# Prefetch hints with the routing bit ahead of every branch of the expert part, and PLE products staged in five buffers in place of two

## The chip, the cores and the metric

The kernel runs on one core of a Trainium2 chip. The metric is the device time of one execution in microseconds (us); the time of a kernel is the median of its timed runs. All durations below are from one profiled execution of the kernel before, by the hardware profiler.

## The reference

One layer of a decoder trunk over 2048 tokens of width 1024, in float32. A mixer (a gated MLP over positions and a gated recurrence) comes first, then a mixture of experts, then a per-layer embedding (PLE) gate and a final norm. The part that the change touches is the mixture and the PLE product:

```python
def hier_moe(h, w_grp, w_exp, w1, w3, w2):
    # top-1 group of 4, then top-2 experts of the 8 inside it: 32 experts, 2048 tokens x 2
    ...
    def expert_block(args):
        xb, e = args
        return (jax.nn.silu(xb @ w1[e]) * (xb @ w3[e])) @ w2[e]

    ybuf = lax.map(expert_block, (buf.reshape(n_blk, MOE_BLOCK, D), blk_e)).reshape(P, D)
    contrib = ybuf[dest] * w_s[:, None].astype(xt.dtype)
    out = jax.ops.segment_sum(contrib, tok_s, num_segments=T)
    return out.reshape(B, S, D)
...
        x = x + merged @ w_out[i]
        h = rmsnorm(x, g_ffn[i])
        x = x + hier_moe(h, w_grp[i], w_exp[i], w1[i], w3[i], w2[i])
        h = rmsnorm(x, g_ple[i])
        x = x + jax.nn.sigmoid(h @ w_pg[i]) * (p[i] @ w_ple[i])
    return rmsnorm(x, g_final)
```

w1 and w3 of an expert are 1024 x 512 each, w2 is 512 x 1024, so an expert brings 6.29 MB of weights. `p[i] @ w_ple` is 2048 x 256 by 256 x 1024; it depends on no routing.

## The kernel before

The program is straight-line code, unrolled, except for the branches named here. Its stages, one behind the other: the mixer with the routing; a stretch in which the routing table is scattered to HBM (`tab_d`), read back (`tokidx`), and the rows of the first experts are gathered; the 32 experts; the final tiles.

**The experts.** Each expert takes its first 128 tokens with split products: ACT makes `ehi` (a rounded copy of a weight piece), DVE makes `elo` (the rest), and PE multiplies three products of two halves each, `P0` to `P7` for the eight pieces of w1 and w3 (L903, six matmuls a piece), then `B0` to `B3` for w2 (L935). `ehi` and `elo` have five buffers each (`SPL`). `x` (L877) and `y` (L881) split the tokens' columns `xr`, which `X` (L852) turns out of the gathered `rows`. The order is written out by hand in the string `PART`: one pass of it for an expert has the second half of the expert before (`S T G B Y`), the first half of this one (`P`, with `h`, `l`, `v`, `u` for ehi and elo), and the first splits of the next one (`X x y H L`). Inside one engine the instructions run in this order and no other.

**The branches.** At the end of each pass stands, on every engine, `tc.If` on a bit of the routing code (L1095): has the expert more than 128 tokens? If so, `some(0)` does the next 32 with plain products (L948, a transpose L954, L959); a second bit (L1097) asks for the next 32, `some(1)`; a third (L1099) for the rest in a loop (`rest`). The bodies are nested, and stand in the program between the branch and its target, so a branch that is taken (the bit is clear) jumps over code that is in the program but isn't run. In this run's data 16 of the 32 experts skip at L1095, 13 run `some(0)` alone and skip at L1097, and 3 run both and skip at L1099. A skipped or finished body ends with a wait of each engine's own semaphore in the block behind the jump.

**Queues.** The sequencer of PE (PEq) hands instructions to the PE queue ahead of their execution. [...] SP issues the weight loads (w13r L718, w2r L725) and the stores of PLE products in order; POOL issues the gathers (L837) and the scatters `y_d` (L844).

**PLE.** `ple()` (L1006 to L1014) makes twelve of the sixteen tiles of `p @ w_ple`: for each, PE runs 4 matmuls (L543), ACT copies the two halves into `po` (L544), and SP stores it to `ple_d` (L1013). `po` has two buffers, under the tag "y" that the experts' outputs use later. PE's transposes of `praw` (L535) give the columns. The work is interleaved by `FILL` with the routing, and what is left stands ahead of the first expert. Here the scheduler, by its own estimates, sets the order on each engine.

Of the kernel before, what the change touches and what calls it, by code (L numbers as in the profile page):

```python
# [8 lines left out]
F32 = mybir.dt.float32  # L9
F32R = mybir.dt.float32r  # L10
# [4 lines left out]
AF = mybir.ActivationFunctionType  # L15
OP = mybir.AluOpType
AX = mybir.AxisListType
SYNC = mybir.DependencyInfo(mybir.DependencyClass.Sync, mybir.DependencyReason.DATA)
NOSYNC = mybir.DependencyInfo(mybir.DependencyClass.NoSync, mybir.DependencyReason.DATA)
PSUM = bass.MemoryType.PSUM  # L20
# [2 lines left out]
T = 2048  # L23
D = 1024
# [10 lines left out]
EPG = 8  # L35
# [7 lines left out]
SPL = 5  # L43
W2B = 8
HGRN = "forget0 R query0 R decay0 og0 R og20 forget1 R att0 query1 state0 decay1 og1 read0 R og21 forget2 R R R norm0 att1 query2 decay2 og2 state1 forget3 read1 R norm1 att2 og22 og3 query3 R state2 decay3 R G og23 att3 G read2 G state3 norm2 G read3 norm3"
PART = "S P0 P1 h2 l2 h3 l3 T G P2 B0 X h4 l4 B1 h5 l5 x B2 h6 l6 y B3 h7 l7 P3 P4 Y v0 u0 P5 v1 u1 P6 H0 L0 P7 H1 L1"
ORDER = [EPG * g + i for i in range(EPG) for g in (0, 1, 3, 2)]
EARLY = 4
E0 = 0, 0, 2, 2
# [25 lines left out]
def tile_hybrid_block(ctx: ExitStack, tc: tile.TileContext, a, out):  # L75
# [3 lines left out]
    x = a["x"][0]  # L79
# [66 lines left out]
    with ExitStack() as fin, ExitStack() as route_ctx, ExitStack() as moe_ctx:  # L146
# [477 lines left out]
        def route(b, pt, rs):  # L624
# [5 lines left out]
            gm = rt.tile([128, MB], F32, name="gm")  # L630
            vec.tensor_reduce(gm, gl, axis=AX.X, op=OP.max)
            gmb = gm[:, :, None].to_broadcast([128, MB, NG])
# [3 lines left out]
            gw = rt.tile([128, MB], F32, name="gw")  # L636
            vec.tensor_reduce(gw, gq, axis=AX.X, op=OP.max)
            for m in range(MB):
# [28 lines left out]
            for j in range(2):  # L667
                vec.tensor_reduce(rk[:, :, j], oh[:, :, j], axis=AX.X, op=OP.add)
            ad = rt.tile([128, MB, 2], I32, name="ad")
# [15 lines left out]
            pg = rt.tile([128, MB], F32, name="pg")  # L685
            vec.tensor_reduce(pg, ge, axis=AX.X, op=OP.add)
            vec.reciprocal(pg, pg)
# [115 lines left out]
        code = sm.tile([1, 3, NG], F32, name="code")  # L803
        for j, top in enumerate((128.0, 160.0, 192.0)):
            bit = C["bits"][:, j]
# [5 lines left out]
        xe = moe_ctx.enter_context(tc.tile_pool(name="xe", bufs=1, side="right", reuse_waits="tile"))  # L811
# [194 lines left out]
        def ple():  # L1006
            for m4 in range(1, NB):
                if m4 == 3:
                    ple_turn(praw, pturn[3])
                for m in range(MB):  # L1010
                    o = xe.tile([128, D], F32, name="po", tag="y", bufs=2)
                    ple_tile(m, pturn[m4], o)
                    nc.sync.dma_start(ple_d[m4 * MB + m], o)  # L1013
                    yield  # L1014
# [29 lines left out]
        r13.append(moe_ctx.enter_context(tc.tile_pool(name="r13b", bufs=4, side="right", reuse_waits="tile")))  # L1044
        xl = moe_ctx.enter_context(tc.tile_pool(name="xl", bufs=1, reuse_waits="tile"))
        codes_r, loads = [], []

        def load(src, top):
            done = len(nc.cur_bb.bb.instructions)
# [14 lines left out]
        with tc.manual_schedule():  # L1064
            for i in range(NE + 1):
                was, now, then = (ex[j] if 0 <= j < NE else None for j in (i - 1, i, i + 1))
                if then:
                    then.w13, then.w2 = list(load_expert(i + 1))[-1]
                    if i == 0:
                        first.clear()  # L1070
                elif now:
                    nc.sync.dma_start(gple, a["g_ple"][0].rearrange("(n p) -> p n", p=128))
                    for k2 in range(PGE):
                        load_pg(k2)
                    praw = xe.tile([128, MB, PLE], F32, name="praw0", tag="rows", bufs=2)
                    ple_rows(0, praw)
                if i + 2 < NE:
                    ex[i + 2].fetch()
                if now is None:
                    ple_turn(praw, pT)  # L1080
                for word in PART.split():
                    name, k = word[0], int(word[1:] or 0)
                    if name in "STGBY":
                        if was:
                            getattr(was, name)(*([k] if name == "B" else []))
                    elif name in "HLXxy":
                        if then:
                            getattr(then, {"H": "hi", "L": "lo"}.get(name, name))(*([k] if name in "HL" else []))
                    elif now:
                        if name in "vu":  # L1090
                            k += KT
                        getattr(now, {"h": "hi", "l": "lo", "v": "hi", "u": "lo"}.get(name, name))(k)
                if now:
                    code, bit = codes_r[now.e // EPG], 8 ** (now.e % EPG)
                    with tc.If((code & bit) != 0):  # L1095
                        now.some(0)
                        with tc.If((code & 2 * bit) != 0):  # L1097
                            now.some(1)
                            with tc.If((code & 4 * bit) != 0):  # L1099
                                now.rest()  # L1100

        moe_ctx.close()
# [197 lines left out]
```

## Time and profile before

| | us |
|---|---|
| median of three timed runs | 2516.56 (2515.40 to 2517.98) |
| the profiled execution | 2525.01 |
| its span in the trace | 2523.3 |
| mean granted TensorE clock of it | 0.981 |
| PE busy | 2385.7 (95% of the span) |

PE is the engine that is nearly always busy, so the time is that of its work, of its idle gaps, and of stretches in which its clock is granted at half. A row of the waits says which instruction of PE waited, and for whom; "PEq" as the one waited for is PE's own sequencer, which had not yet handed the instruction over. [...]

### The profile page before, as it was taken

The numbers are of one execution on the slowest core, as the hardware profiler recorded it, in microseconds if no ns is written. First come the engines' busy times: TensorE is split into PE (matmuls) and PEld (weight loads), VectorE is DVE, ScalarE is ACT, GpSimd is POOL, SyncE is SP. The second block draws the span as 40 slices with busy tenths as digits, with TensorE's granted clock in tenths as the row PEclk, the third lists the DMA queues.
The fourth block names the chain that finished last, engine by engine and source line by source line (L and its number), as shares of the span: only waits on it lengthen the run. The fifth ranks groups of instructions, "written<-read, shape, count | busy, mean of one in ns | idle before, by whom it ended". The sixth has DMA issues, their size and how long they took to land. (4 is left out here: it accounts for less than half of the span.)

```text
span 2523.3 us, 37662 instructions
## 1 busy us (share of the span) xinstructions
PE 2385.7 (95%) x13676; PEld 1917.9 (76%) x13676; DVE 1449.5 (57%) x2505; ACT 1281.2 (51%) x1964; POOL 390.5 (15%) x371
## 2 busy tenths in 40 slices
PE   7999999999999999999999988898888988888998
PEld 6898898988898878988888746665656666665887
DVE  6563455663446644447634536575665757565776
ACT  6763345753347633357523335464554646554443
POOL 0000000100000100001000234242333334311000
PEclk9999999999999999999999999999999999999999
DMA  5333452334442234432435368786876869784553
GB/s 167 93 88 101 123 155 84 81 101 129 124 127 68 84 113 130 145 94 79 134 96 160 130 241 314 262 327 241 298 292 254 317 253 346 275 306 180 212 217 125
DMA packets 313092, 445.82 MB, mean 177 GB/s; under 512 B 32442, under 2 KB 231174, under 8 KB 310752
## 3 DMA queue, kind: packets, MB, share of 16 engines
q1 hardware_dynamic: 290272, 385.68, 45.5%
q0 software_dynamic: 22528, 56.46, 6.2%
q8 instruction: 158, 2.59, 0.4%
q14 instruction: 134, 1.10, 0.1%
HBM read 401.87 MB, written 51.02 MB: 179 GB/s over the span
## 5 line engine op out<-in xcount | busy, mean ns | idle before, releaser
L178 DVE TENSOR_TENSOR wlo<-wraw,whi 128x512 fp32r<-128x512 f32 x445 | 305.4, 689 | 423.6 <-ACT whi L177 395.8
L177 ACT ACTIVATE whi<-wraw 128x512 fp32r<-128x512 f32 x448 | 281.2, 628 | 519.2 <-PE pa L202 321.4
L201 PE MATMUL pa<-h,whi 128*128 128x512 f32 x1024 | 403.4, 394 | 0.0
L202 PE MATMUL pa<-h,whi 128*128 128x512 f32 x1024 | 399.9, 391 | 0.0
L203 PE MATMUL pa<-h,wlo 128*128 128x512 f32 x1024 | 399.4, 390 | 0.0
L894 DVE TENSOR_TENSOR elo<-w13r,ehi 128x1024 fp32r<-128x1024 f32 x256 | 308.2, 1217 | 96.5 <-ACT ehi L888 80.9
L888 ACT ACTIVATE ehi<-w13r 128x1024 fp32r<-128x1024 f32 x256 | 262.8, 1053 | 96.4 <-PE pa L903 90.6
L837 POOL DMA_INDIRECT rows<-h_d,tokidx x192 | 234.1, 1219 | 270.4 <-issue 84.0
L903 PE MATMUL pa<-ehi,xhi 128*128 128x512 f32 x512 | 190.2, 454 | 65.5 <-PEq L1095 21.0
L201 PEld LDWEIGHTS pa<-h,whi 128*128 128x128 f32 x1024 | 192.4, 188 | 42.0 <-issue 0.7
L203 PEld LDWEIGHTS pa<-h,wlo 128*128 128x128 f32 x1024 | 192.3, 188 | 40.9
L202 PEld LDWEIGHTS pa<-h,whi 128*128 128x128 f32 x1024 | 192.4, 188 | 39.4
L903 PEld LDWEIGHTS pa<-ehi,xhi 128*128 128x128 f32 x512 | 98.5, 203 | 110.8 <-ACT ehi L888 42.3
L903 PE MATMUL pa<-ehi,xlo 128*128 128x512 f32 x512 | 171.3, 417 | 1.1 <-issue 1.1
L903 PE MATMUL pa<-elo,xhi 128*128 128x512 f32 x512 | 169.6, 414 | 1.4 <-issue 1.1
L221 PE MATMUL pa<-whi,h 128*128 128x256 f32 x512 | 146.2, 286 | 0.1
L222 PE MATMUL pa<-wlo,h 128*128 128x256 f32 x512 | 145.3, 284 | 0.0
L223 PE MATMUL pa<-whi,h 128*128 128x256 f32 x512 | 145.3, 284 | 0.0
L221 PE MATMUL pa<-whi,hi 128*128 128x256 f32 x512 | 143.6, 280 | 0.0
L222 PE MATMUL pa<-wlo,hi 128*128 128x256 f32 x512 | 143.3, 280 | 0.0
L223 PE MATMUL pa<-whi,lo 128*128 128x256 f32 x512 | 143.1, 279 | 0.0
L903 PEld LDWEIGHTS pa<-elo,xhi 128*128 128x128 f32 x512 | 102.5, 200 | 27.1 <-issue 1.6
(320 smaller groups left out, 4544.0 us busy)
## 6 DMA issues: line engine op xcount, KB each, us to landing
w13r<-in_w_dram SPq DMA_DIRECT2D x256, 512.0 KB
wraw<-in_w_in_dram SPq DMA_DIRECT2D x320, 256.0 KB
w2r<-in_w_dram SPq DMA_DIRECT2D x128, 512.0 KB
wraw<-in_w_out_dram SPq DMA_DIRECT2D x64, 256.0 KB
yt<-y_d SPq DMA_DIRECT2D x16, 1024.0 KB
xt<-in_x_dram SPq DMA_DIRECT2D x32, 256.0 KB
wraw<-in_w_up_a_dram SPq DMA_DIRECT2D x32, 256.0 KB
wraw<-in_w_up_b_dram SPq DMA_DIRECT2D x32, 256.0 KB
```

The source lines that it names most:

```text
L177: whi = act.activation(hi, raw, AF.Copy)
L178: wlo = (pool if n < POOLG else vec).tensor_tensor(lo, raw, hi.bitcast(F32), op=OP.subtract)
L201: pe.matmul(ps, hi[:, k4], xhi, start=k == 0, stop=False)
L202: pe.matmul(ps, hi[:, k4], xlo, start=False, stop=False)
L203: pe.matmul(ps, lo[:, k4], xhi, start=False, stop=k == n_k - 1)
L221: pe.matmul(o, xhi[:, s], hi[:, k2], start=st, stop=False, skip_group_check=True)
L222: pe.matmul(o, xhi[:, s], lo[:, k2], start=False, stop=False, skip_group_check=True)
L223: pe.matmul(o, xlo[:, s], hi[:, k2], start=False, stop=k == n_k - 1, skip_group_check=True)
L837: ins = pool.indirect_dma_start(out=g[:, q], out_offset=None, in_=h2_d, in_offset=bass.IndirectOffsetOnAxis(ap=idx[:, at:at + 1], axis=0), ...
L888: act.activation(t, self.raw(k), AF.Copy)
L894: vec.tensor_tensor(t, self.raw(k), hi.bitcast(F32), op=OP.subtract)
L903: pe.matmul(self.ph[n], xp[:, k], w[:, n], start=k == 0 and w is hi and xp is self.xhi, stop=k == KT - 1 and xp is self.xlo)
```

## The change

Two edits. The first adds hints: `tc.mark_branch_hint_location` names a branch by its label, and passes a register that tells at run time whether the branch will be taken: 0 that it will (its target is then to be fetched), 1 that it won't. `(code & bit) // bit` is just the routing bit, which is 0 where the body is skipped. Word `n` of `PART` gives the hint for L1095 on POOL and SP at the head of a pass; word `m` gives it on PE, ACT and DVE ahead of P5. Within the bodies PE alone gets hints for L1097 ("most", at the head of `some(0)`) and L1099 ("beyond", at the head of `some(1)`). The second puts `po` into the five buffers of the tag "elo" that the experts use, in place of the two of "y".

```diff
-PART = "S P0 P1 h2 l2 h3 l3 T G P2 B0 X h4 l4 B1 h5 l5 x B2 h6 l6 y B3 h7 l7 P3 P4 Y v0 u0 P5 v1 u1 P6 H0 L0 P7 H1 L1"
+BUSY = [mybir.EngineType.PE, mybir.EngineType.Activation, mybir.EngineType.DVE]
+QUEUED = [mybir.EngineType.Pool, mybir.EngineType.SP]
+PART = "n S P0 P1 h2 l2 h3 l3 T G P2 B0 X h4 l4 B1 h5 l5 x B2 h6 l6 y B3 h7 l7 P3 P4 Y v0 u0 m P5 v1 u1 P6 H0 L0 P7 H1 L1"
...
-                    o = xe.tile([128, D], F32, name="po", tag="y", bufs=2)
+                    o = xe.tile([128, 2, 512], F32R, name="po", tag="elo", bufs=SPL)
+                    o = o.rearrange("p n c -> p (n c)").bitcast(F32)
...
+        def skip(label, code, bit, engines):
+            tc.mark_branch_hint_location(label, (code & bit) // bit, engines=engines)
...
+                    elif now and name in "nm":
+                        code, bit = codes_r[now.e // EPG], 8 ** (now.e % EPG)
+                        skip(f"more{i}", code, bit, {"n": QUEUED, "m": BUSY}[name])
...
-                    with tc.If((code & bit) != 0):
+                    with tc.If((code & bit) != 0, preferred_fallthrough_block=True, label=f"more{i}"):
+                        skip(f"most{i}", code, 2 * bit, BUSY[:1])
                         now.some(0)
-                        with tc.If((code & 2 * bit) != 0):
+                        with tc.If((code & 2 * bit) != 0, preferred_fallthrough_block=True, label=f"most{i}"):
+                            skip(f"beyond{i}", code, 4 * bit, BUSY[:1])
                             now.some(1)
-                            with tc.If((code & 4 * bit) != 0):
+                            with tc.If((code & 4 * bit) != 0, preferred_fallthrough_block=True, label=f"beyond{i}"):
                                 now.rest()
```

PE at the end of the first expert's pass, before: the last of P7's matmuls, the branch, and the bodies behind it.

```order
L903 MATMUL pa<-ehi,xlo 128x512 x2
L1050 TENSOR_LOAD codes
L1095 REGISTER_ALU
L1095 COMPARE_AND_BRANCH
L948 MATMUL pb<-w13r,xr 32x256 x32
L954 MATMUL pb<-ident,sg 128x128
L959 MATMUL pb<-w2r,st 32x256 x16
L1097 REGISTER_ALU
L1097 COMPARE_AND_BRANCH
```

PE there after the change (the line numbers have moved: L1103 was L1095, L1106 was L1097, L905 was L903; L1306 and L1052 are the hint and its arithmetic). The first rows are those ahead of P5.

```order
L1056 TENSOR_LOAD codes
L1052 REGISTER_ALU
L1306 BRANCH_PREFETCH_HINT
L905 MATMUL pa<-ehi,xhi 128x512 x2
...
L1103 REGISTER_ALU
L1103 COMPARE_AND_BRANCH
L1052 REGISTER_ALU x2
L1306 BRANCH_PREFETCH_HINT
L950 MATMUL pb<-w13r,xr 32x256 x32
L956 MATMUL pb<-ident,sg 128x128
L961 MATMUL pb<-w2r,st 32x256 x16
L1106 COMPARE_AND_BRANCH
```

The rows left out are the 18 matmuls of P5, P6 and P7: the hint for the outer branch stands 18 matmuls ahead of it, that for the inner one stands at the head of the body, 49 matmuls ahead. The blocks themselves stand where they stood.

SP around the reading of the routing table, before (`ple_d_67` is the store of the first of the twelve PLE tiles, `ple_d_68` of the second, and so on; `tokidx` is the table, which is there only once it has been scattered).

```order
L1013 DMA ple_d_67<-po 128x1024
L1013 DMA ple_d_68<-po 128x1024
L829 DMA tokidx<-tab_d 32x6x32 x3
L1013 DMA ple_d_69<-po 128x1024
L1013 DMA ple_d_70<-po 128x1024
L829 DMA tokidx<-tab_d 32x6x32
```

SP there after the change.

```order
L1016 DMA ple_d_67<-po 128x1024
L1016 DMA ple_d_68<-po 128x1024
L1016 DMA ple_d_69<-po 128x1024
L1016 DMA ple_d_70<-po 128x1024
L1016 DMA ple_d_71<-po 128x1024
L1016 DMA ple_d_72<-po 128x1024
L831 DMA tokidx<-tab_d 32x6x32
L1016 DMA ple_d_73<-po 128x1024
L831 DMA tokidx<-tab_d 32x6x32 x3
L1016 DMA ple_d_74<-po 128x1024
```

Six stores stand ahead of the first read of the table now, in place of two; the last three of the twelve (`ple_d_76` to `ple_d_78`) stand between the first weight loads of the second expert, where the last six stood before.

DVE ahead of the first expert after the change (before, four `elo` of the first expert stood ahead of the `traw` copy and both `xr` ahead of the fifth `elo`).

```order
L833 COPY traw<-tokidx 128x192
...
L1042 COPY yi<-traw 32x32 x4
L896 TENSOR_TENSOR elo<-w13r,ehi 128x1024 x2
L854 STREAM_TRANSPOSE xr<-rows 128x1536
L896 TENSOR_TENSOR elo<-w13r,ehi 128x1024 x2
L883 TENSOR_TENSOR xlo<-xr,xhi 128x1024
L854 STREAM_TRANSPOSE xr<-rows 128x1536
L896 TENSOR_TENSOR elo<-w13r,ehi 128x1024 x3
```

The first five `elo` tiles follow the last five PLE tiles in the same five buffers, so each of them now waits for the store of one PLE tile.

## Rows read from the trace of the kernel before

**Rows 1.** The page: the queue of PE's instructions; packets, MB, share of the DMA engines.

```profile
q8 instruction: 158, 2.59, 0.4%
```

**Rows 2.** Windows: PLE stretch, experts; start:end, length, busy of each engine, PEclk, DMA share, GB/s.

```profile
1441.00:1498.00 57.00, 46.51 (x120) 23.74 (x119) 20.26 (x37) 18.84 (x29) 30.60 (x26) 0.88 0.67 240
1498.00:2291.00 793.00, 703.10 (x4081) 491.03 (x4079) 499.75 (x472) 433.76 (x535) 267.51 (x224) 0.95 0.78 287
```

**Rows 3.** Waits of PE, 1441 to 2330: instruction, waited for, total us, times, longest.

```profile
PE pa L903 <- PEq L1095: 21.0, 9, 2.7
PE pa L903 <- issue: 19.3, 8, 5.6
PE pa L903 <- PEq L1097: 14.2, 5, 3.2
...
PE pa L543 <- ACT po L544: 10.2, 3, 3.8
PE pa L903 <- ACT ehi L888: 8.1, 3, 2.8
...
PE pa L903 <- ACTq L1097: 3.0, 5, 0.6
...
PE pa L903 <- ACTq L1099: 2.0, 3, 0.7
```

**Rows 4.** Groups by line, PE, 1498 to 2291: P's first products, busy, mean ns, idle before.

```profile
L903 PE MATMUL pa<-ehi,xhi 128*128 128x512 f32 x498 | 185.4, 455 | 65.5 <-PEq L1095 21.0 <-issue 17.1 <-PEq L1097 14.2
```

**Rows 5.** The branches of L1095 on PE's sequencer: duration ns min/median/max, first and last start.

```profile
L1095 PEldq COMPARE_BRANCH  x32: 78/1804/6362, 1498.3 to 2286.8; - x32
```

**Rows 6.** Line L1095, window 2114 to 2120: one taken branch on PE's sequencer.

```profile
L1095 PEldq COMPARE_BRANCH  x1: 6177/6177/6177, 2116.1 to 2116.1; - x1
```

**Rows 7.** Timeline of PE across that branch: start, us, instruction, idle before and releaser.

```profile
2119.74 0.63 PE L903 MATMUL pa<-ehi,xlo 128*128 128x512 f32 x2
2122.62 1.19 PE L903 MATMUL pa<-ehi,xhi 128*128 128x512 f32 x2 [2.26 <-PEq L1095]
```

**Rows 8.** Windows of two passes of experts without a body, with and without stall.

```profile
2116.00:2137.90 21.90, 19.64 (x74) 14.33 (x73) 15.93 (x15) 13.65 (x16) 10.80 (x9) 0.92 0.90 318
2137.90:2158.00 20.10, 17.93 (x74) 13.00 (x73) 15.63 (x15) 13.55 (x16) 8.14 (x8) 1.00 0.97 361
```

**Rows 9.** The last branch of L1095, and the timeline of PE behind it.

```profile
L1095 PEldq COMPARE_BRANCH  x1: 3520/3520/3520, 2286.8 to 2286.8; - x1
```

**Rows 10.** Timeline of PE behind that last branch.

```profile
2291.62 1.06 PE L535 MATMUL pb<-ident,praw 128*128 128x128 f32 x8 [0.56 <-ACT g L908]
```

**Rows 11.** The branches of L1097 on PE.

```profile
L1097 PEldq COMPARE_BRANCH  x29: 75/193/3934, 1504.9 to 2271.2; - x29
```

**Rows 12.** Timeline of PE at two jumps of L1097, the long and the short kind.

```profile
2271.41 0.73 PE L903 MATMUL pa<-ehi,xhi 128*128 128x512 f32 x2 [2.87 <-PEq L1097]
...
1817.32 0.74 PE L903 MATMUL pa<-ehi,xhi 128*128 128x512 f32 x2 [0.60 <-ACTq L1097]
1819.20 0.73 PE L903 MATMUL pa<-elo,xhi 128*128 128x512 f32 x2 [1.14 <-issue]
```

**Rows 13.** Timeline of PE, PLE stretch: 16 + 32 + 16 matmuls, then the first expert.

```profile
1447.43 10.05 PE L543 MATMUL pa<-wple,pT 128*128 128x512 f32 x16 [3.84 <-ACT po L544]
1460.65 15.44 PE L543 MATMUL pa<-wple,pT 128*128 128x512 f32 x32 [3.16 <-ACT po L544]
1479.28 8.83 PE L543 MATMUL pa<-wple,pT 128*128 128x512 f32 x16 [3.19 <-ACT po L544]
1487.55 1.04 PE L903 MATMUL pa<-ehi,xhi 128*128 128x512 f32 x2
```

**Rows 14.** Timelines of ACT and DVE, PLE stretch.

```profile
1474.00 1.06 ACT L877 ACTIVATE xhi<-xr 128x1024 fp32r<-128x1024 f32 x1 [4.14 <-DVE xr L852]
...
1461.62 0.26 DVE L831 COPY traw<-tokidx 128x192 int32<-128x192 int32 x1 [12.98 <-DMA tokidx<-tab_d]
...
1483.90 1.78 DVE L852 STREAM_TRANSPOSE xr<-rows 128x1536 f32<-128x1536 f32 x1 [9.94 <-DMA rows<-h_d,tokidx]
```

More of the change, by code (lines that the diff above doesn't have):

```diff
@@ L1093, in tile_hybrid_block @@
                 if now:
-                    code, bit = codes_r[now.e // EPG], 8 ** (now.e % EPG)
-                    with tc.If((code & bit) != 0):
+                    with tc.If((code & bit) != 0, preferred_fallthrough_block=True, label=f"more{i}"):
+                        skip(f"most{i}", code, 2 * bit, BUSY[:1])
                         now.some(0)
-                        with tc.If((code & 2 * bit) != 0):
+                        with tc.If((code & 2 * bit) != 0, preferred_fallthrough_block=True, label=f"most{i}"):
+                            skip(f"beyond{i}", code, 4 * bit, BUSY[:1])
                             now.some(1)
-                            with tc.If((code & 4 * bit) != 0):
+                            with tc.If((code & 4 * bit) != 0, preferred_fallthrough_block=True, label=f"beyond{i}"):
                                 now.rest()
```

## The prediction, made before the changed kernel ran

> **What bounds the kernel now.** I read the windows by stage first, then PE's waits, then the branches, then the timeline around one of them. In the expert part PE is busy for 703 of 793 us, ACT and DVE for 434 and 500, and the DMA engines for 0.78 of the time [rows 2]: PE sets the pace, and what it loses there is 90 us of gaps and the clock. The granted clock is 0.95 on average, which over 793 us is 0.05 x 793 = 40 us of work at full rate.
>
> The gaps have one main place. Of the idle time before PE's first products of a piece, 65.5 us [rows 4], all is found again in the waits [rows 3]: 21.0 us (9 times) on PEq L1095, 17.1 us of "issue" (6 times; the other 2 of the 8, 2.2 us together, stand inside a pass, such as the 1.14 us in [rows 12]), 14.2 us (5) on PEq L1097, 8.1 us (3) put down to an ehi, 3.0 us (5) on ACTq L1097 and 2.0 us (3) on ACTq L1099. The counts fit the branches: 15 = 9 + 6 outer jumps to the next pass, 38.1 us; 13 = 5 + 3 + 5 inner jumps, of which eight are long, 22.3 us, mean 2.79, and five short, mean 0.60; three jumps of L1099, mean 0.67.
>
> Why a jump costs this is seen in one of them. The sequencer came to the branch at 2116.1 and stayed on it for 6.18 us [rows 6], to 2122.3; PE worked off what it had been handed, to 2120.37, then sat idle for 2.26 us [rows 7]. So the sequencer was 4.2 us ahead, and the branch took longer than that lead. A branch that isn't taken takes 78 ns [rows 5, 11]. PE's instructions come in packets of 2.59 MB / 158 = 16 KB [rows 1], and I read the 6.2 us as the fetch of the target's packet behind the weight traffic. At the last branch it took 3.52 us [rows 9], less than the lead, and PE still idled 0.56 us [rows 10], since the block behind the jump waits for PE itself: that is what a hidden jump leaves.
>
> **The change, part by part.**
>
> Outer hint on PE. It stands 18 matmuls ahead of the branch. At 17.93 / 74 = 0.242 us a matmul [rows 8] that is 4.4 us, and the sequencer keeps its lead over PE in between. A fetch that needs the whole 6.2 us is then over 1.8 us after the branch is reached, 2.4 us before PE runs dry. So 14 ordinary jumps (38.1 - 5.6 = 32.5 us, mean 2.32) fall to 0.56: 14 x 1.76 = 24.6 us. The fifteenth, the 5.6 us [rows 3], has more in it than the branch; I take 1.8 of it as well. Together 26.4 us; bounds 0 (the fetch starts no earlier) and 38.1 - 15 x 0.56 = 29.7.
>
> Inner hint. It stands 49 matmuls ahead, the whole body. Eight long jumps at 2.79 fall to the 0.60 of the short ones: 2.19 each. One of them may have its stall in the packet behind the target, as the 1.14 us of [rows 12] show there can be one, so 7 x 2.19 = 15.3 us; bounds below, at the rivals. The hint for L1099 can win nothing: those three already idle 0.67.
>
> The clock. A pass with a stall ran at 0.92 and had PE busy for 19.64 us, the next without at 1.00 and 17.93 for the same 74 matmuls [rows 8]: 1.71 us per stall. 40 us / 23 long stalls (15 + 8) = 1.73, the same price: the half-rate stretches belong to the long stalls. Behind 0.60 us of idle the first pair took 0.74 us, behind 2.26 us 1.19 [rows 12, 7]. With 21 of 23 stalls shortened to about 0.6 that gives up to 36 us; I take 30, since a gap stays at each jump and some may still bring the clock down; bounds 0 and 40. Of the 30, 20 belong to the outer jumps, 10 to the inner.
>
> The hints' own cost. On PE each is two to four register instructions, near the 78 ns of a branch that falls through, at most 0.3 us on a sequencer that is 4.2 us ahead: nothing. Without that cover it is 0.3 x 51 (32 passes and 19 bodies) = 15 us. ACT, DVE, POOL and SP have room by their busy time [rows 2]; on POOL the hint stands between a gather and the scatter behind it, on SP behind the weight loads and ahead of the branch, and neither has a DMA behind it that PE waits for in the same pass.
>
> PLE. PE has 64 matmul records left from 1443.6 on (eight tiles), and runs them with three gaps of 3.84, 3.16 and 3.19 us, all for `po` [rows 13, 3], at 0.88 of the clock over these 57 us [rows 2]. The first expert starts at 1487.55 because PE is behind with them; its xhi was there at 1475.06 [rows 14]. With five buffers and six stores ahead of the table's read, PE runs on: 64 x 15.44 / 32 = 31 us, to 1474.5. What is late next is xlo. DVE now comes to it behind the third and fourth `elo`, which wait for the stores of the tenth and eleventh tile, and these stand behind weight loads that wait for the gathered rows: I put xlo's end at 1481.5 and P0 at 1482, 5.5 us earlier. The second `xr` at 1483.90 [rows 14] then stands ahead of the fifth `elo` on DVE: 1485.7 + 1.2 = 1486.9, and P4 wants it at 1482 + 4 x 1.4 = 1487.6, just enough. Bounds: +9 if the stores land at once, -3 if the table's read waits for the sixth store (traw was copied at 1461.62, and each PLE tile is 8 x 0.48 = 3.9 us, so the sixth is only some 4 us ahead of it), which moves all gathers.
>
> DMA. A pass without a body needs 0.90 x 21.9 = 19.7 or 0.97 x 20.1 = 19.5 us of the DMA engines [rows 8], and PE would need 17.93 + 0.56 = 18.5. On average a pass is 793 / 32 = 24.8 us and its DMA 0.78 of that, so only several such passes in a row are held: 3 us given back, bounds 0 and 16 x 1.1 = 18.
>
> **Sum.** 26.4 + 15.3 + 30 + 5.5 - 3 = 74 us off the profiled 2525.0 gives 2451. That execution is 8.45 us above the median of 2516.56, so the forecast is 2442 us; by the bounds of the terms 2428 to 2460.
>
> **Rivals.**
>
> Inner hint without effect (a target that lies too far, or a packet that is replaced again before it is used): the 15.3 and 10 us stay, 2442 + 25 = 2467. For it: within a body the next packets are fetched in order anyway, and eight of 13 jumps missed. Against: nothing in the trace tells a hint in a body from one ahead of it.
>
> The inner hint drops a packet that is needed. In five short jumps, three of L1099 and three branches of L1097 that fell through, the packets needed were there without a hint. If the hinted packet takes the place of the body's next one, each of these eleven bodies stalls instead, for about 2.19 + 1.71 = 3.9 us: 43 us, so 2485, or 2510 if the other eight gain nothing either. For it: eight long jumps within some hundred instructions mean that little is held ahead.
>
> [...]
>
> No effect at all: the fetch is asked for but starts only behind the weight traffic or at the branch. Then only PLE is left, 2516.6 - 5.5 = 2511, with its bounds 2507 to 2520.
>
> Slower: the hinted packet takes the place of the one that PE's sequencer is on. Then the stall of a skipped pass only moves from behind P7 to a place inside P5 to P7, (a gain of 0), and each of the 19 bodies pays 3.9 us: 74 us, against 25 saved at the inner jumps and 5.5 at PLE: 2516.6 + 43 = 2560. It is slower than before from (25 + 5.5) / 3.9 = 8 stalled bodies on. Against: an engine that throws out what it runs would be a strange design.
>
> **How the numbers follow.** The forecast with its bounds has 0.56, the inner hint without effect 0.15 (2460 to 2475), the dropped packet 0.15 (2475 to 2512), no effect 0.08 (2507 to 2520), slower 0.05, still faster than 2428 0.01. 2428 to 2503 holds 0.56 + 0.15 + 0.11 = 0.82. A measurement tells 0.2% from nothing, 5 us: faster means under 2511.5. That is 0.56 + 0.01 + 0.15 + 0.14 and nearly none of no effect, 0.86; same 0.09; slower 0.05.
>
> **What would show it.** Right: the waits of PE on PEq L1095 and on issue at P0 gone from 38 to some 8 us; the longest branch of L1095 near or under 4 us; the inner ones all under 0.5 us; PEclk 0.99 or 1.00 over the experts; P0 of the first expert near 1482; passes without a body at 18.5 to 19.7 us. Wrong: PE idle in the middle of `some` or of P5 to P7 for two us or more (a dropped packet); branches as long as before (no effect); P0 waiting for a weight tile or DMA share at 1.0 over a whole row of passes (DMA is the bound); the table's copy later than 1462 (PLE lost).

## The result, and the profile after

| | before | after |
|---|---|---|
| median | 2516.71 us (2515.40 to 2517.98, 4 runs) | 2480.82 us (2473.56 to 2482.06, 4 runs) |
| ratio to before, 95% interval | | 0.9851 (0.9831 to 0.9871) |
| the profiled execution | 2525.01 us | 2473.56 us |
| its mean granted clock | 0.981 | 0.992 |

The change takes 36 us off the median; the interval of the ratio allows 32 to 43. The two profiled executions are 51.5 us apart, which is more, because the one of before lies above its median and the one of after below its own. The account that follows is between these two executions.

Two windows, first of the kernel before, then of the kernel after: the experts (from the first body to the end of the last expert's pass) and the final tiles. The columns are those of [rows 2].

```profile
1499.20:2291.60 792.40, 701.96 (x4076) 490.34 (x4076) 498.55 (x471) 433.03 (x534) 267.51 (x224) 0.95 0.78 287
2291.60:2523.30 231.70, 215.00 (x984) 170.71 (x984) 160.62 (x389) 100.42 (x218) 14.66 (x18) 0.97 0.48 181
```

```profile
1493.60:2241.80 748.20, 684.67 (x4077) 475.66 (x4076) 495.53 (x469) 432.28 (x534) 273.70 (x224) 0.99 0.81 302
2241.80:2471.80 230.00, 213.30 (x984) 169.97 (x984) 160.57 (x389) 100.45 (x218) 14.50 (x18) 0.98 0.49 183
```

The experts start 5.6 us earlier (1499.2 to 1493.6), take 44.2 us less, and the final tiles 1.7 us less: 51.5 us. Of the 44.2 us in the experts, PE's idle time is 27.0 (792.40 - 701.96 = 90.4 before, 748.20 - 684.67 = 63.5 after) and PE's busy time 17.3. The matmuls are the same, so the 17.3 us are the clock: 0.95 before, 0.99 after.

PE's waits in the stretch from PLE to the end of the experts, after (L1103 was L1095, L1106 was L1097, L905 was L903):

```profile
PE pa L905 <- ACTq L1106: 10.8, 9, 3.5
PE pa L905 <- ACT ehi L890: 7.6, 3, 2.6
PE pa L905 <- DVE xlo L883: 6.8, 1, 6.8
PE pa L905 <- issue: 6.5, 2, 3.4
...
PE pa L905 <- DVEq L1103: 4.2, 14, 0.3
PE pa L905 <- PEq L1103: 4.2, 14, 0.3
PE pa L905 <- ACTq L1103: 3.1, 1, 3.1
...
PE pa L905 <- PEq L1106: 2.1, 1, 2.1
```

Set against [rows 3], the 27.0 us of idle time come apart like this. **Outer jumps**: 38.1 us before; now 4.2 + 4.2 + 3.1 = 11.5, so 26.6 less. **Inner jumps** of L1106: 14.2 + 8.1 + 3.0 = 25.3 before; now 10.8 + 7.6 + 2.1 = 20.5 (13 jumps, 9 + 3 + 1), so 4.8 less. **Stalls inside a pass**: two of 2.2 us together before; now two of 6.5 us together, so 4.3 more. That is 27.1.

The outer branches on PE's sequencer, after (compare [rows 5]), and one of them with PE's timeline across it (compare [rows 6, 7]):

```profile
L1103 PEldq COMPARE_BRANCH  x32: 75/227/3347, 1489.5 to 2237.0; - x32
```

```profile
L1103 PEldq COMPARE_BRANCH  x1: 1256/1256/1256, 2061.4 to 2061.4; - x1
```

```profile
2065.02 0.63 PE L905 MATMUL pa<-ehi,xlo 128*128 128x512 f32 x2
2065.95 0.47 PE L905 MATMUL pa<-ehi,xhi 128*128 128x512 f32 x1 [0.30 <-PEq L1103]
2066.72 0.51 PE L905 MATMUL pa<-ehi,xhi 128*128 128x512 f32 x1 [0.30 <-DVEq L1103]
2067.06 0.62 PE L905 MATMUL pa<-elo,xhi 128*128 128x512 f32 x2
```

The branch was reached at 2061.4 and done at 2062.7. PE had work until 2065.65, so the branch is hidden; the gap of 2.26 us of [rows 7] is two of 0.30 now, one ahead of P0's first matmul and one behind it. The hint itself was reached at 2056.2, and one packet of q8 comes between it and the branch, from 2060.2 to 2061.2. The longest outer branch is 3.35 us (6.36 before), still shorter than the lead of some 4.2 us.

The inner branches did not change their kind. After, and the timeline of PE at one of them:

```profile
L1106 PEldq COMPARE_BRANCH  x29: 71/200/3440, 1499.2 to 2222.9; - x29
```

```profile
1642.46 1.93 PE L961 MATMUL pb<-w2r,st 128*32 128x256 f32 x32 [0.43 <-issue]
1647.91 1.22 PE L905 MATMUL pa<-ehi,xhi 128*128 128x512 f32 x2 [3.51 <-ACTq L1106]
```

The longest is 3.44 us (3.93 in [rows 11]), and of the 13 jumps that skip there, 6 still leave PE idle for over 2 us (7 before, and an eighth for 1.94). In five of the six the branch itself takes 3.0 to 3.4 us. The one shown is the sixth: its branch took 0.36 us, and PE sat for 3.51 us at the block behind it. The pair that follows takes 1.22 us; the clock was granted at 0.50 there (1647 to 1653).

The packets of PE's instruction queue (q8; 155 packets, 2.54 MB, so 16 KB each) tell the jumps apart. In the kernel before, one of them falls into each of the 23 branches of L1095 and L1097 that took over 2 us. After the change, counted from the outer branch to the inner one, the five with the long branch have none; the eight with a short branch have one or two. In the kernel before, which has no hints, the five short jumps have one each, so a short jump can also come of a packet that came without a hint; three of the eight others have one too. Two packets come in three bodies after the change and in none of the kernels without inner hints (before, e1, e3, e7), so the inner hint may have been followed in those three; one of them is the jump of 3.51 us.

PLE and the first expert, PE's timeline (compare [rows 13]), then DVE's:

```profile
1472.73 0.73 PE L905 MATMUL pa<-ehi,xhi 128*128 128x512 f32 x2 [1.63 <-ACT xhi L879]
...
1480.72 1.22 PE L905 MATMUL pa<-ehi,xlo 128*128 128x512 f32 x2 [6.80 <-DVE xlo L883]
```

```profile
1474.80 1.23 DVE L896 TENSOR_TENSOR elo<-w13r,ehi 128x1024 fp32r<-128x1024 f32 x1 [4.71 <-DMA ple_d<-po]
1478.31 1.23 DVE L896 TENSOR_TENSOR elo<-w13r,ehi 128x1024 fp32r<-128x1024 f32 x1 [2.29 <-DMA ple_d<-po]
1479.45 1.22 DVE L883 TENSOR_TENSOR xlo<-xr,xhi 128x1024 fp32r<-128x1024 f32 x1
```

PE no longer waits for `po`. It reaches the first expert at 1472.73 instead of 1487.55, and then waits 6.8 us for `xlo`, which on DVE stands behind two `elo` that wait for stores of PLE tiles.

### The profile page after: what moved, and what is told of

It reads as the page before. It is cut to its first block, busy times and chain, and to the rows that moved or that the text cites. A ratio compares the mean times of both kernels' runs of the same rounds, so it can differ in the third digit from the quotient of the medians.

```text
span 2471.8 us, 38160 instructions
## 1 busy us (share of the span) xinstructions
PE 2362.5 (96%) x13676; PEld 1901.6 (77%) x13676; DVE 1449.1 (59%) x2505; ACT 1281.4 (52%) x1964; POOL 393.2 (16%) x371
## 3 DMA queue, kind: packets, MB, share of 16 engines
q8 instruction: 155, 2.54, 0.4%
## 5 line engine op out<-in xcount | busy, mean ns | idle before, releaser
L839 POOL DMA_INDIRECT rows<-h_d,tokidx x192 | 240.0, 1250 | 286.2 <-issue 100.4
L905 PE MATMUL pa<-ehi,xhi 128*128 128x512 f32 x512 | 185.9, 440 | 36.0 <-ACTq L1106 10.8
L905 PE MATMUL pa<-ehi,xlo 128*128 128x512 f32 x512 | 164.8, 403 | 6.8 <-DVE xlo L883 6.8
L905 PE MATMUL pa<-elo,xhi 128*128 128x512 f32 x512 | 164.8, 403 | 6.8 <-issue 6.5
L905 PEld LDWEIGHTS pa<-ehi,xhi 128*128 128x128 f32 x512 | 94.9, 193 | 84.7 <-ACTq L1106 15.1
L905 PEld LDWEIGHTS pa<-ehi,xlo 128*128 128x128 f32 x512 | 98.9, 193 | 34.0 <-DVE xlo L883 7.2
```

The source lines that it names most:

```text
L839: ins = pool.indirect_dma_start(out=g[:, q], out_offset=None, in_=h2_d, in_offset=bass.IndirectOffsetOnAxis(ap=idx[:, at:at + 1], axis=0), ...
L905: pe.matmul(self.ph[n], xp[:, k], w[:, n], start=k == 0 and w is hi and xp is self.xhi, stop=k == KT - 1 and xp is self.xlo)
```

## The experiments

All kernels compute the whole output. "Before" ran beside each on the same chip; ratios are to that. The diffs are against the changed kernel. A jump is called long where PE is idle for over 2 us at it.

**PLE alone (e1).** All hints are taken out, and with them the labels of the branches and their `preferred_fallthrough_block`; `po` keeps its five buffers.

```diff
-PART = "n S P0 P1 ... Y v0 u0 m P5 v1 u1 P6 H0 L0 P7 H1 L1"
+PART = "S P0 P1 ... Y v0 u0 P5 v1 u1 P6 H0 L0 P7 H1 L1"
...
-                        skip(f"most{i}", code, 2 * bit, BUSY[:1])
...
-                            skip(f"beyond{i}", code, 4 * bit, BUSY[:1])
```

> The PLE products in five buffers, no hints. In the profiles the first body starts 5.6 us earlier after the change (1499.21 to 1493.64 us). If that is the PLE edit alone and nothing gives it back: 2516.7 - 5.6 = 2511 us, stalls of PE at the outer jumps as before (38 us over 15), clock over the experts 0.95. Rival: the gain is taken back by the stalls that follow (another phase of weight traffic): 2514 to 2519 us.

Measured: 2513.04 us (10 runs), ratio 0.9996 (0.9977 to 1.0015). The profile has the step, the times cannot tell it from none. PE, with no hint anywhere, meets the same wait for `xlo` as in the whole change:

```profile
1481.64 1.22 PE L903 MATMUL pa<-ehi,xlo 128*128 128x512 f32 x2 [6.86 <-DVE xlo L881]
```

**Hints alone (e2).** `po` goes back to two buffers.

```diff
-                    o = xe.tile([128, 2, 512], F32R, name="po", tag="elo", bufs=SPL)
-                    o = o.rearrange("p n c -> p (n c)").bitcast(F32)
+                    o = xe.tile([128, D], F32, name="po", tag="y", bufs=2)
```

> All hints, PLE in two buffers as before. If the two edits add up: 2480.8 + 5.6 = 2486 us, PE idle at the 15 outer jumps some 11 us in place of 38, clock over the experts 0.98 to 0.99, first P0 near 1487.5 us. Rival: the stages interact, and the hints alone give the whole 36 us: 2481 us or less.

Measured: 2489.53 us, ratio 0.9889 (0.9860 to 0.9917). The hints bring nearly all of the gain. The whole change is 8.7 us below this one and PLE alone 3.9 below before: the 5.6 us that the profile shows lie between, but the second of these is within the noise.

**Outer hints without inner ones (e3).**

```diff
-                        skip(f"most{i}", code, 2 * bit, BUSY[:1])
...
-                            skip(f"beyond{i}", code, 4 * bit, BUSY[:1])
```

> The full change without the inner hints (those at the head of the two bodies). In the profile of the changed kernel no packet was fetched between an inner hint and its branch wherever the jump was long. Theory: inner hints do nothing where they stand, so this is 2480.8 us within 5 us (only the position of the code in the packets moves), with 4 to 8 long inner jumps of about 2.6 us idle. Rival: they drop a packet that is needed next, in the stalls of 3 us behind some jumps; then this is faster by 8 to 13 us (2468 to 2473).

Measured: 2482.73 us, ratio 0.9866 (0.9839 to 0.9892), against 2480.82 of the whole change: the inner hints of the change are worth nothing that can be measured. 9 of the 13 inner jumps are long. PE's waits:

```profile
PE pa L905 <- ACT ehi L890: 13.1, 5, 2.8
...
PE pa L905 <- PEq L1105: 11.8, 4, 3.0
```

These are the nine (L1105 is the inner branch here), 24.9 us.

**The inner hint later (e4).** It stands behind the first 32 matmuls of the body, 17 ahead of its branch, as near as the outer hint to its own. The hint for L1109 moves likewise.

```diff
-                        skip(f"most{i}", code, 2 * bit, BUSY[:1])
-                        now.some(0)
+                        now.some(0, lambda: skip(f"most{i}", code, 2 * bit, BUSY[:1]))
```

> The full change with the inner hints moved from the head of the body to behind its first 32 matmuls, 17 matmuls ahead of the inner branch, about as far as the outer hint is from the outer branch. Theory of place: a hint at the head, right behind the outer branch, is lost, one near its branch works: each taken inner branch has one fetched packet between hint and branch, all 13 idles at about 0.6 us, none over 1, time 2480.8 - 6 x 2.0 - some 5 of clock = 2464 us (2458 to 2470). Theory of state: the outer hint, which said not taken in these passes, uses the mechanism up; then nothing changes, 4 to 8 long jumps stay, 2476 to 2486 us.

Measured: 2475.18 us, ratio 0.9844 (0.9816 to 0.9872). 8 long inner jumps stay, the longest branch is 3.83 us:

```profile
L1106 PEldq COMPARE_BRANCH  x29: 71/200/3829, 1498.7 to 2217.2; - x29
```

So neither of the two places of the hint in the body is the reason. The 5.6 us against the whole change are about its scatter from run to run; this run has no stall of the 3.4 us kind inside a pass.

**Inner hints without outer ones (e5).**

```diff
-PART = "n S P0 P1 ... Y v0 u0 m P5 v1 u1 P6 H0 L0 P7 H1 L1"
+PART = "S P0 P1 ... Y v0 u0 P5 v1 u1 P6 H0 L0 P7 H1 L1"
```

> The full change without the outer hints on any engine: only the inner hints on PE at the head of the bodies are left (and PLE in five buffers). Theory of state: an outer hint that says not taken stands in the way of the inner one; without it the inner hints fetch, each long inner jump (5 to 9 of 13, about 2.7 us) falls to 0.6, while the 15 outer stalls of 38 us are back: 2511 - 8 x 2.1 - 5 of clock = 2489 us (2485 to 2495). Theory that a hint inside a body never acts here: no fetch between hint and branch, jumps as before, 2508 to 2516 us like the PLE edit alone.

Measured: 2490.14 us, ratio 0.9883 (0.9864 to 0.9901). Here the same inner hints work: 2 long inner jumps instead of 6 to 9, while the outer stalls are back. PE's waits (L1104 outer, L1107 inner):

```profile
PE pa L905 <- PEq L1104: 33.3, 15, 2.8
...
PE pa L905 <- ACTq L1107: 7.0, 11, 0.7
PE pa L905 <- PEq L1107: 3.1, 1, 3.1
...
PE pa L905 <- ACT ehi L890: 2.6, 1, 2.6
```

The queue of PE's instructions says the same. First the whole change, from the inner hint to its branch in one body, then this kernel in the body of the same expert; the rows are queue, packets, MB, share, and in the first there is none of q8 between q0 and the next heading:

```profile
...
q0 software_dynamic: 329, 0.80, 23.1%
issues: line engine op xcount, KB each, median us to landing
```

```profile
...
q0 software_dynamic: 166, 0.40, 11.6%
q8 instruction: 1, 0.02, 0.7%
```

In the whole change no packet follows the inner hint of this body, and its branch takes 3.32 us; without the outer hint one packet follows, and the branch takes 0.35. So it is over all 13 bodies of this kernel: the eleven with a short branch have a packet, the two with a long one have none.

**The outer hint always "taken" (e6).** On PE the outer hint says that the body will be skipped, for every expert (the third bit is clear in this data); that is wrong for 16 of 32. There is no inner hint.

```diff
-                        skip(f"more{i}", code, bit, {"n": QUEUED, "m": BUSY}[name])
+                        skip(f"more{i}", code, bit, {"n": QUEUED, "m": BUSY[1:]}[name])
+                        if name == "m":
+                            skip(f"more{i}", code, 4 * bit, BUSY[:1])
...
-                        skip(f"most{i}", code, 2 * bit, BUSY[:1])
...
-                            skip(f"beyond{i}", code, 4 * bit, BUSY[:1])
```

> As with outer hints alone, but PE's outer hint always says taken (it is given a bit of the code that is 0 for every expert), so that it is wrong in the 16 passes that run a body; no inner hints. The target of the outer jump lies next to that of the inner one. If the hinted packet takes the place of the next one in order (few packets held): in the bodies that run across the end of a packet PE stalls for 2 to 3 us in the body or at its fall-through (4 to 7 of 16), the others jump with 0.6 us: time 2470 to 2482. If many packets are held: no stall in bodies, all inner jumps at 0.6 us, 2482.7 - 9 x 2.1 - 5 = 2459 us (2454 to 2466). If the hint is only followed when it is right, nothing changes: 2480 to 2486.

Measured: 2452.41 us (2450.52 to 2453.00), ratio 0.9736 (0.9719 to 0.9754); 28.4 us below the whole change. The inner branches, the waits, and the window of the experts (L1105 outer, L1107 inner):

```profile
L1107 PEldq COMPARE_BRANCH  x29: 88/197/496, 1499.6 to 2199.2; - x29
```

```profile
PE pa L905 <- ACTq L1107: 8.4, 13, 0.8
```

```profile
1493.40:2218.10 724.70, 677.71 (x4078) 470.48 (x4076) 494.86 (x470) 431.88 (x535) 269.89 (x224) 1.00 0.84 312
```

All 13 inner jumps are short now, mean 0.65, though no hint names them. An inner exit ends at the same block as the outer jump, and that the packet of that block is already there is a reading of it, for which the packets counted below speak. In this run the bodies do not pay for it. PE through one body to the next P0:

```profile
1635.54 3.66 PE L950 MATMUL pb<-w13r,xr 128*32 128x256 f32 x64
1639.92 0.33 PE L956 MATMUL pb<-ident,sg 128*128 128x128 f32 x1 [0.72 <-DVE sg L955]
...
1643.22 0.72 PE L905 MATMUL pa<-ehi,xhi 128*128 128x512 f32 x2 [0.60 <-ACTq L1107]
```

The two waits are those of any body: 13.7 us over 19 for `sg`, 8.4 over 13 at the inner jumps. In this pass the sequencer reaches the hint at 1626.1, the outer branch at 1631.4 and the inner one at 1641.2. One packet came for PE between the hint and the outer branch, and one between the two branches:

```profile
q8 instruction: 1, 0.02, 1.2%
```

```profile
q8 instruction: 1, 0.02, 0.7%
```

The body ran without a stall and its jump was short, so nothing here shows that either packet was dropped before it was used. In seven of the 13 bodies a packet comes behind the hint, none inside the body, and the inner jump is short all the same. From its rows the prediction put a stall of 3.9 us on each body in which the hinted packet takes the place of a needed one. Sixteen such bodies would have cost 62 us here, and the run is 28 us faster: that stall did not come in this run.

**The outer hint on PE alone (e7).**

```diff
-                        skip(f"more{i}", code, bit, {"n": QUEUED, "m": BUSY}[name])
+                        skip(f"more{i}", code, bit, BUSY[:1])
```

Word `n` and the inner hints are out too.

> Outer hints on PE alone, none on ACT, DVE, POOL and SP, no inner hints. The prediction gave the other engines' hints nothing, as those engines have room: 2482.7 us within 5, as with outer hints on all five. Rival: ACT and DVE stall at their own branches, and P0 then waits for ehi or elo: 2487 to 2500.

Measured: 2474.78 us, ratio 0.9827 (0.9810 to 0.9844): 8 us below e3, which differs by the hints of the four other engines, though the same time was expected. The intervals of the two ratios overlap. So these hints gain nothing, and whether they cost something is open.

**`xlo` ahead of the third `elo` (e8).** The whole change, and on DVE the first expert's `xlo` stands ahead of the `elo` that wait for stores.

```diff
+                ins = vec.tensor_tensor(t, self.raw(k), hi.bitcast(F32), op=OP.subtract)
+                if k > 1 and y0:
+                    after(ins, y0.pop())
...
-        ex[0].y()
+        y0.append(ex[0].y())
```

> The full change, and on DVE xlo of the first expert ordered ahead of its third and fourth elo, which wait for the stores of PLE tiles. In the changed kernel P0 stops for 6.8 us after four matmuls, for xlo, and runs at half rate for 10 us behind it. If that order is the cause: P0 goes through at 1473, P2 waits for the third elo until some 1476, P4 for the fifth until 1482; the first body at 1489 to 1491 in place of 1493.6, and 2476 to 2478 us for 2480.8. Rival: the stores set the end anyway (the fifth elo waits for the last of them), nothing changes.

Measured: 2475.38 us, ratio 0.9824 (0.9801 to 0.9846), within the scatter of the whole change. PE's timeline:

```profile
1475.41 1.06 PE L907 MATMUL pa<-ehi,xlo 128*128 128x512 f32 x2
...
1482.03 0.73 PE L907 MATMUL pa<-elo,xhi 128*128 128x512 f32 x2 [1.08 <-DVE elo L896]
...
1485.46 0.90 PE L907 MATMUL pa<-elo,xhi 128*128 128x512 f32 x2 [1.76 <-DVE elo L896]
...
1492.32 1.93 PE L952 MATMUL pb<-w13r,xr 128*32 128x256 f32 x32
```

The 6.8 us of waiting for `xlo` are gone, so the order on DVE was their cause. The first body starts only 1.3 us earlier (1493.64 before the edit): 2.84 us come back as waits for the `elo` that were passed, and pairs of matmuls start 0.86 us apart (1475.41 to 1477.12, 1486.16 to 1488.72), as they do in the changed kernel where the granted clock was 0.50 (1476 to 1486); where it was 1.00 there (1486.5 to 1493) they start 0.47 apart.

**Two inner hints (e9).** A second inner hint is added in each body; in the order that comes out it stands on PE one matmul behind the first. The hint for L1109 moves as in e4.

```diff
                         skip(f"most{i}", code, 2 * bit, BUSY[:1])
-                        now.some(0)
+                        now.some(0, lambda: skip(f"most{i}", code, 2 * bit, BUSY[:1]))
```

> The full change with two inner hints in a row in each body, the second one matmul behind the first (outer hints as in the change, with the routing bit). With the outer hints in the program no long inner jump had a packet fetched ahead of it, without them (inner hints alone) most had. Theory that a hint which says not taken swallows exactly one hint behind it: the second inner hint is followed, q8 fetches between hint and branch, all 13 inner idles near 0.6 us, 2460 to 2468 us. Rival: it stands in the way of every hint up to the next taken jump, or the cause is another: 4 to 9 long jumps stay, 2473 to 2484 us.

Measured: 2478.40 us (2 runs), ratio 0.9841 (0.9820 to 0.9862); 7 long inner jumps. The theory that the outer hint uses up one hint behind it and no more had forecast none, and is not borne out. PE also idles six times, 2.5 us in all, in the middle of the first matmuls of a body, which it does nowhere in the changed kernel.

**The always-taken hint at the head of the pass (e10).** As e6, but at word `n`, 82 matmuls ahead of the branch. The diff is against e6.

```diff
-                        if name == "m":
+                        if name == "n":
                             skip(f"more{i}", code, 4 * bit, BUSY[:1])
```

> The outer hint on PE that always says taken, put at the head of the pass instead of ahead of P5: 82 matmuls ahead of the branch instead of 18 (ACT, DVE, POOL and SP hints with the routing bit, no inner hints, PLE in five buffers). If the hinted packet is kept while the packets of a pass go by: the branch is served from it, no branch over 0.6 us, the time as with the late hint, 2450 to 2455. If it is given up for one of the packets that come in order: the outer stalls of 2 us come back in most passes that cross a packet's end (some 8 to 12 of 15) and the inner ones with them, 2475 to 2500.

Measured: 2473.48 us, ratio 0.9821 (0.9803 to 0.9838): 21 us slower than e6. The inner branches are as short as in e6 (under 0.5 us), and PE idles 0.9 to 1.4 us at them (0.6 to 0.8 in e6; the next hint now stands behind each jump). What is longer is the bodies: the 16 of them, each from its first matmul to the next P0, take 165.3 us in all, 143.8 in e6, and that is the whole difference. The same body as above:

```profile
1637.51 3.67 PE L950 MATMUL pb<-w13r,xr 128*32 128x256 f32 x53
1641.51 1.06 PE L950 MATMUL pb<-w13r,xr 128*32 128x256 f32 x11 [0.33 <-issue]
...
1646.85 0.72 PE L905 MATMUL pa<-ehi,xhi 128*128 128x512 f32 x2 [0.90 <-ACTq L1107]
```

From the body's start to the next P0 it is 9.34 us, 7.68 in e6, and PE idles for 0.33 us in the middle of the body's first matmuls, on an issue that no other engine held up. The largest loss, 6.8 us in one body, has another place: PE waits for `sg`, and ahead of that ACT stood idle.

```profile
1837.72 0.47 PE L956 MATMUL pb<-ident,sg 128*128 128x128 f32 x1 [5.60 <-DVE sg L955]
```

```profile
1837.07 0.28 ACT L954 ACTIVATE sg<-pb 128x128 f32<-128x128 f32 x1 [8.84 <-remote]
```

What ACT waited for is not in the trace. That the hinted packet is kept to the end and a packet of the body comes late, the rival of the dropped packet, would fit the first kind of loss: a packet of q8 comes between the outer and the inner branch in ten of the 13 bodies, in six of 13 in e6. It is argued, not shown, and how many packets PE holds was not measured.

**All that helped, together (e11).** On PE alone, one always-taken hint per pass ahead of P5, no other hint; `xlo` first; `po` in five buffers.

```diff
-                        skip(f"more{i}", code, bit, {"n": QUEUED, "m": BUSY}[name])
+                        skip(f"more{i}", code, 4 * bit, BUSY[:1])
```

> What the runs point to: on PE alone one hint a pass, ahead of P5, that always says taken; no hint on the other engines, none in the bodies; PLE in five buffers with xlo of the first expert ahead of its third elo. Always taken gave 2452 us, xlo first some 3 to 5 us at the first expert, the hints on the other four engines at best nothing: 2446 to 2450 us. Rival: the 3 to 5 us are lost at the weights of the second expert: 2452.

Measured: 2450.96 us (2449.46 to 2456.50, 5 runs), ratio 0.9735 (0.9718 to 0.9752). It beats both kernels, the changed one by 30 us, and cannot be told from e6. In its profile the first body starts 3.7 us earlier than in e6, at 1490.23, but the 16 bodies take 152.8 us, 9.0 more than in e6, with PE idle in the middle of their first matmuls:

```profile
PE pb L952 <- issue: 3.5, 6, 0.8
```

e6 has no such wait, and the hint stands in the same place. So the loss in the bodies is not set by the lead of the hint alone; its cause is open.

**The outer hint never "taken" (e12).** e5 with an outer hint on PE that says "not taken" for every expert. The question is whether any outer hint, even one that asks for no target, makes the inner one fail.

```diff
-                        skip(f"more{i}", code, bit, {"n": QUEUED, "m": BUSY}[name])
+                        tc.mark_branch_hint_location(f"more{i}", (code & 4 * bit) // (4 * bit) + 1, engines=BUSY[:1])
```

> Inner hints alone plus one outer hint a pass on PE, ahead of P5, that always says not taken (wrong in the 16 passes that skip). It differs from the run with inner hints alone by that hint only. There 11 of 13 inner jumps were short and two long, at 2490.1 us. Theory that a hint which says not taken stands in the way of the one behind it: no packet comes between an inner hint and its branch, 5 to 9 long inner jumps of 2.7 us return, and the outer stalls stay as they were: 2490 + 5 x 2.1 + 4 of clock = 2504 us (2499 to 2512). Rival: the cause is another, the inner jumps stay at 2 or 3 long ones, 2486 to 2495 us.

Measured: 2494.75 us (6 runs), ratio 0.9922 (0.9895 to 0.9949); 4 long inner jumps, against 2 in e5 and 6 to 9 where the outer hint is the routing bit. Neither answer comes out clearly, and the reason why inner hints are not followed stays open.

## Why the prediction was right or wrong, point by point

**Direction and range.** Faster, and 2480.8 lies in 2428 to 2503. It is 39 us above the 2442 that was forecast, outside the bounds of the forecast itself (2428 to 2460) and of the rival without inner hint (2460 to 2475). The band it falls in was held open for the dropped packet, which did not occur in the bodies; that the whole range holds it is luck. Two steps make up the difference: the inner hint with its clock, and the last line of the sum.

**The outer hint, right.** Forecast 26.4 us of idle time; the waits give 38.1 - 11.5 = 26.6. The cause is as described: the hint was reached some 5.2 us ahead of the branch (4.4 was forecast), the longest branch is 3.35 us against a lead of some 4.2, fourteen jumps at 0.30 ahead of P0 and 0.30 behind its first matmul. The waits leave a little out: between the two gaps PE runs one matmul alone for 0.47 us, the time in which a pair goes through otherwise, so some 0.2 us more is lost at each jump, 3 us in all, and 23 to 24 are really won.

**The inner hint, wrong.** This is the step that failed: "Eight long jumps at 2.79 fall to the 0.60 of the short ones", 15.3 us with 10 of clock. The idle time at inner jumps fell by 4.8 us, and stalls inside a pass took 4.3 back. The rival that the hint is without effect is what happened, with its forecast of 2467 on the median; e3 shows it, since without inner hints the time is the same. The reasons given for that rival, a target too far or a packet replaced again, do not account for it: e4 moves the hint to 17 matmuls and nothing comes of it, and e5 fetches the packet from the same place 49 matmuls ahead once no outer hint stands in front. "Nothing in the trace tells a hint in a body from one ahead of it" was true; what the runs tell apart is whether an outer hint stands ahead (6 to 8 long jumps in the kernels with both hints) or not (2 in e5). Why the one hint stands in the way of the other is not known.

**The size of that term, right.** e6 makes all inner jumps short by another way, and its profiled execution is 2452.26 us, 21.3 below that of the change, where the term said 25.3. PE's idle time at inner jumps is 8.4 us in e6, 16.9 less than in the kernel before (forecast 15.3), and the clock gave 7.0 (forecast 10). So the prices of a jump and of its half-rate stretch were fairly read, and the assumption that this hint would buy them was not borne out. That the sum against the profile, 2451, meets e6 to 1 us is partly luck: the clock gave 24.3 in all and not 30, which the DMA term of 3 us that was not needed and the 2.2 us of stalls inside a pass that are gone nearly make up.

**The clock, right in kind.** Forecast 20 us with the outer jumps and 10 with the inner ones. PE's busy time fell by 17.3 in the changed kernel, where the outer jumps are served, and by another 7.0 in e6 (684.67 to 677.71, the clock at 1.00), where the inner ones are too.

**The dropped packet.** In the changed kernel it did not occur in the bodies: none has PE idle in the middle of the first matmuls of `some`. In e6 it did not occur either. Its sign, PE idle in the middle of `some`, though for 0.8 us and less, is seen in e9, e10 and e11, and bodies 21.5 and 9.0 us longer than in e6 in e10 and e11; that a dropped packet is the cause is not shown. What did occur was not foreseen as a cost, though [rows 12] hold a small one of it, of 1.14 us: PE starts behind the jump and stops again a few matmuls on. It happened twice in the changed kernel, 6.5 us together. One of them, PE behind a jump of L1109 (L1099 before):

```profile
1749.69 0.73 PE L905 MATMUL pa<-ehi,xhi 128*128 128x512 f32 x2 [0.75 <-ACTq L1109]
...
1755.43 0.50 PE L905 MATMUL pa<-elo,xhi 128*128 128x512 f32 x1 [3.38 <-issue]
```

In that gap one packet of q8 comes, from 1753.0 to 1754.0; that PE waited for it is a reading.

**PLE, right on the profile.** Forecast P0 at 1482 with `xlo` at 1481.5, 5.5 us. Measured: PE starts P0 at 1472.73, waits for `xlo` until 1480.72, and the first body is 5.6 us earlier. e8 confirms the reason for the remaining wait. By times alone (e1) the step is within the scatter.

**The DMA engines, nothing.** Forecast 3 us given back. In the changed kernel PE's only wait for a split weight that does not stand at a jump is one of 0.3 us, and in e6 the experts take 724.7 us, 68 less than in the kernel before, at a DMA share of 0.84.

**The slower case and the hints' own cost, nothing.** In the changed kernel no pass stalls in P5 to P7, and sixteen wrong hints cost nothing in e6.

**From the profile to the median, wrong.** The last line took off 8.45 us since the execution of before lay that much above its median. That assumed that the change keeps the offset. The profiled execution of after is 7.3 us below its own median. On the profile the forecast was 2451 against 2473.56, 22.5 us too low: 14.8 are idle time (the inner jumps, and the stalls inside a pass, which the sum did not have) and 12.7 the clock, less the 4.7 of the DMA term and the final tiles. The other 16 us of the 39 are this line. Where the offset comes from was not tested. In e6 and e11, where no long inner jump is left, the profiled time and the median agree to 0.2 us, but in e9, with seven, they do too.

## What to carry to other kernels

Where an engine stalls at jumps over unrolled code, give the branch hint on the engine that sets the pace, shortly ahead of the branch (here 18 matmuls, some 5 us on PE's sequencer; 82 matmuls, 14 us, was 21 us worse), and count for each jump whether its wait is gone; a hint that is given is not yet a packet that is fetched. If inner exits end at the same place as the outer jump, one hint for that place, always "taken", served them all here. Where it was wrong it cost nothing in e6 and some 9 us in the bodies of e11, so measure the bodies too. Read the price of the stall from the pass with its clock, not from the gap alone: here 1.7 us of half-rate work came with 2.3 to 2.8 us of idling.

## What the runs showed of the hardware that was not expected

- A hint given for a nested branch behind the hint of the branch around it was mostly not followed: of 13 inner jumps, 6 to 9 stayed long in every kernel whose outer hint was the routing bit, with or without inner hints (7 in the kernel before, with no hints at all), 4 behind an outer hint of "not taken", 2 with no outer hint. Each number is from one trace. Why is open.
- A hint that names the wrong way cost nothing measurable 18 matmuls ahead of its branch in e6; 82 matmuls ahead the program was 21 us slower, all of it in the bodies. With the hint at 18 and no hints on the other engines (e11) the bodies were 9 us longer than in e6.
- Behind a jump at which PE idled only 0.75 us it idled again for 3.38 us, nine matmuls on; one packet of PE's queue lands 1.5 us before it goes on. Read as the next packet coming late, this is a second price of a jump; the first, in [rows 7], was 2.26 us.
